# High parts of the woven stage's weights: rounded by a casting transfer of GpSimd's queue instead of by ScalarE, with rings of 5 high and 3 low slots

## The chip, the cores and the metric

The kernel runs on one core of one Trainium2 chip. The metric is the device time of one execution in microseconds (us); of several runs the median is taken. The core's engines are TensorE (PE, with PEld for its weight loads), VectorE (DVE), ScalarE (ACT), GpSimd (POOL) and SyncE (SP), which here issues most transfers; each engine works through its own queue in order and waits there for semaphores of the others.

## The reference, cut to what matters

One layer of a hybrid backbone on 256 latent and 256 context tokens, width 2048, in float32: modulated RMSNorm, one input projection, two token mixers beside one another (a bidirectional RWKV-7 with 16 heads, a bidirectional chunked gated DeltaNet with 8 heads), a gated merge of both, an output projection, a residual, and a SwiGLU network with 5632 hidden columns.

```python
h = modulate(rmsnorm(x, norm1_w[layer]), sh1, sc1)
hc = modulate(rmsnorm(ctx, norm1_w[layer]), csh1, csc1)
...
rw, cv, z, ab, gt = jnp.split(h @ w_in, IN_SPLITS, axis=-1)
...
m = jax.nn.sigmoid(g_a) * (o_a @ p_a) + jax.nn.sigmoid(g_b) * (o_b @ p_b)
return m @ w_out
...
x = x + gt1 * y
x = x + gt2 * swiglu(modulate(rmsnorm(x, norm2_w[layer]), sh2, sc2),
                     ffn_w_gate_up[layer], ffn_w_down[layer])
```

The change touches how the weights of `w_in`, `p_a` and part of `p_b` are made ready for the products.

## The kernel before

Large products run on TensorE in the type fp32r, which keeps fewer bits than float32. To keep precision, each weight W and each input X is split in a high part, W rounded to fp32r, and a low part, W minus the high part. A product is then three matmuls: high W by high X, high W by low X, low W by high X.

The kernel has four stages. The first (until about 120 us) makes the modulation and the normed inputs HX and HC (high and low each) and the narrow low-rank columns. The second is the **woven stage** (L164 in the profile), the subject here. The third is the output projection, with the rest of the merge (L1860 to L1862), and the fourth the feed-forward network (L415 to L438).

In the woven stage some thirty generators, each a chain of single operations, are interleaved: `products` (the large products), `prepare`, `grams`, `inverse`, `values` and `scan` for eight pairs of RWKV heads, `features`, `tokens`, `decays`, `head_grams`, `head_inverse` and `head_scan` for eight DeltaNet heads, the merge, and the rest of the modulation (`ada_early`, `ada_rest`). The class `Weave` orders them when the program is built: it keeps a planned time for each engine (a `Lane`) and each generator, always takes the operation that can start earliest by the plan's costs (ties by rank), and emits it. So the order on TensorE, VectorE, ScalarE, GpSimd and SyncE is fixed by a plan whose costs and delays stand in `LAT`; on the chip each engine follows that order and waits where the plan was too hopeful. All of it is recorded under the line of the one call in `Lane.__getattr__`, L164, and loads under L175.

Weights come in **quarters**: 4 of the 16 blocks of 128 rows of a 128-column strip, a tile of 128 x 512 (256 KB). For each quarter two generators run, at a rank ahead of all others:

- `fetch` takes a raw slot from the ring `raws` (3 slots at first; 6 once the early modulation is done with the other three) and has SyncE load the quarter into it.
- `cast` waits for the planned landing, takes a high slot from `his`, has ScalarE round the raw quarter into it (CAST whi<-wraw), takes a low slot from `los`, and has VectorE subtract (TENSOR_TENSOR wlo<-wraw,whi). Then the raw slot goes back, and `products` may use the pair.

The rings `his` and `los` have 4 slots each, the halves of two tiles whi and two tiles wlo. A quarter's 12 or 24 matmuls (latent tokens alone, or latent and context) use both parts; then both slots go back. The loader asks for up to four quarters ahead of the product that runs.

GpSimd has little to do: for each pair it clears edges of a tile (L896, L900), copies and adds the two directions' keys for the bonus (L928, L930, tile bon), and clears the inverse's work tile.

Of the 399 quarters that are cast this way, 344 are of w_in, 32 of pa (p_a) and 23 of pb (p_b); three of the last are gathered from several strips, with columns of 128 elements.

Of the kernel before, what the change touches and what calls it, by code (L numbers as in the profile page):

```python
# [18 lines left out]
P = 128  # L19
# [4 lines left out]
NH = HID // P  # L24
NPAIR = 8
NGH = 8
DECAY = 0.6065306597126334
NHELD, NB = 10, 10
GATES_A, GATES_B = ((36,0,0,0,0,0,0,0),(0,0,0,0,0,4,0,0))

LAT = dict(dma=3.1, v=1.0, s=1.0, hop=dict(e=0.215, v=0.135, s=0.15, g=0.1), slack=0.1, own=0.09, grp=32, crank=-1, cg=4, into=0.14, back=0.2, cross=0.14, stay=0.0, gpace=1.6)
LNEXP = "natural_log_exp_and_others"
SIGM = "sigmoid_and_others"
UNIT = 64 * 64 + 64
# [78 lines left out]
class Lane:  # L113
# [36 lines left out]
    def __getattr__(self, name):  # L150

        def op(out, *a, **k):
            if name == "preload_act_table_set":
                return Op(self, 1.2, lambda: self.engine.preload_act_table_set(out))
            if name == "dma_start":
                return Op(self, 0.6 if self.each > 0.002 else 0.06, lambda: self.engine.dma_start(out, *a))
            mode = base = None
            if name == "transpose" and len(a) == 2:
                cost, mode = 0.109, "full"
            elif name == "matmul":  # L160
                cost, mode = self.product(out, a)
            else:
                cost, base = self.cost(name, out, a, k), (out.offset // out.ap[0][0], out.shape[0])
            return Op(self, cost, lambda: getattr(self.engine, name)(out, *a, **k), mode, base)  # L164
        return op
# [163 lines left out]
def emit(ctx: ExitStack, tc, A, out, dbg=None):  # L329
# [4 lines left out]
    weave = Weave()  # L334
    dq = Loads(Q)
    e, v, s, g = (Lane(x, fixed, each, LAT["own"], LAT["hop"][n]) for x, fixed, each, n in
                  ((E, 0.0, 0.0, "e"), (V, 0.07, 0.00104, "v"), (S, 0.06, 0.0009, "s"), (G, 0.06, 0.0022, "g")))
# [458 lines left out]

    raws, his, los = quarters("wraw", 3, F32), Ring(quarters("whi", 2, F32R)), Ring(quarters("wlo", 2, F32R))
    turns = [itertools.cycle(t) for t in (raws, his.tiles[:], los.tiles[:])]
    raws, spare = Ring(raws[:3]), raws[3:]

    for b in (pib, mmb, psb, psb, mmb, pab):
# [12 lines left out]
    landed = {}  # L814
# [341 lines left out]
    def fetch(parts, i):  # L1156

        for q, part in enumerate(parts):
            raw = yield raws
            landed[i, q] = raw, weave.now + dq(raw[:, :part.shape[1]], part)  # L1160
            weave.ready("asked", i, q)
            yield 0.0

    def cast(parts, i):

        for q, part in enumerate(parts):
            n = part.shape[1]
            yield "asked", i, q
            raw, at = landed.pop((i, q))
            yield max(0.0, at - weave.now)  # L1170
            hi = yield his
            yield s.copy(hi[:, :n], raw[:, :n])
            lo = yield los
            yield v.tensor_sub(lo[:, :n], raw[:, :n], hi[:, :n].bitcast(F32))
            raws.put(raw)
            casts[i, q] = hi, lo
            weave.ready("cast", i, q)
# [16 lines left out]
    def merge_in():  # L1194

        yield "out", NPAIR - 1
        for what in "KV":
            yield what + "gemm", NGH - 1
        oa = hx.tile([P, 2, 8, T], F32R, tag="ch", name="oa")
# [15 lines left out]
    def merge_gates():  # L1215
# [8 lines left out]
        yield w  # L1224
        yield "gram", NGH - 1
        for t in gts:
# [647 lines left out]
    with tc.manual_schedule(engines={mybir.EngineType.PE, mybir.EngineType.DVE, mybir.EngineType.Activation,  # L1874
# [17 lines left out]
        at = (KT - NB) * NGH // CG  # L1892
        acc = mp.tile([P, 1024], F32, name="acc")
        adds = dict(zip((1, 2, 4, 6, 8, 10, 12, 13), range(KT - NLATE, KT)))
        for j in range(KT):
# [7 lines left out]
            k, a = divmod(j, 4)  # L1903
            raw = zap.tile([P, CG, P], F32, tag="wr", name="wr", bufs=2)
# [4 lines left out]
            if j in adds:  # L1909
                i = adds[j]  # L1910
# [25 lines left out]
    with tc.tile_pool(name="fp", bufs=1, reuse_waits="tile") as fp:  # L1936
# [19 lines left out]
        for j in range(NH):  # L1956
# [6 lines left out]
            g = fp.tile([P, T], F32, tag="g", name="g", bufs=2)  # L1963
# [5 lines left out]
            if 2 <= j < 34:  # L1969

                for a in range(2):
                    c = (j - 2) // 2
                    i = 2 * (j % 2) + a
# [120 lines left out]
```

## Time and profile before

| | us |
|---|---|
| profiled execution, its own time | 2182.99 |
| its span | 2181.2 |
| median of 3 runs | 2189.1 |
| the runs | 2182.12, 2189.1, 2189.5 |

| engine | busy us | share of the span |
|---|---|---|
| TensorE matmul | 2104.2 | 96% |
| TensorE weight load | 1973.0 | 90% |
| VectorE | 1551.6 | 71% |
| ScalarE | 1119.0 | 51% |
| GpSimd | 19.3 | 1% |

The share is a mean over stages with different limits, so the stretch of the woven stage is read by itself. The granted clock of TensorE is 0.989 over the span. Matmuls are pipelined: their times overlap, and a busy TensorE can still have short stalls inside.

### The profile page before, as it was taken

The page shows a single profiled execution, that of the slowest core. Times are in us where ns is not written, and L with a number is a line of the kernel's source. Part 1 is how long each engine was busy: PE and PEld are TensorE (multiplying, and loading weights), DVE is VectorE, ACT ScalarE, POOL GpSimd, SP SyncE. Part 2 cuts the span into 40 slices and gives each one's busy share as a digit, 9 for nine tenths or more (in the row PEclk, how much of TensorE's full clock was granted, in tenths as well). Part 3 has the DMA queues.
Part 4 walks back from the last instruction along what each step waited for, and adds up shares of the span by engine and source line. Part 5 has one row for each costly group of instructions (what it writes and reads, how often), then busy time and mean ns, then how long its engine had stood idle before and what let it go on. Part 6 is the DMA issues. An engine that isn't in the chain of part 4 may idle for free.

```text
span 2181.2 us, 59117 instructions
## 1 busy us (share of the span) xinstructions
PE 2104.2 (96%) x24536; PEld 1973.0 (90%) x24536; DVE 1551.6 (71%) x3305; ACT 1119.0 (51%) x2210; POOL 19.3 (1%) x55
## 2 busy tenths in 40 slices
PE   7999999999999999999999998999999999999997
PEld 4987698888898898998989988999999999999997
DVE  4466599889889976898998777865666665554554
ACT  3246654555555556565565664644444444444443
POOL 0000000000000000000000000000000000000000
PEclk9999999999999999999999999999999999999999
DMA  9966756645565564665653745946777776566665
GB/s 385 410 168 198 228 140 180 188 141 154 164 162 154 159 168 142 188 194 169 173 160 105 218 151 178 306 161 216 242 244 239 242 239 209 195 191 194 196 194 163
DMA packets 276813, 431.14 MB, mean 198 GB/s; under 512 B 119872, under 2 KB 137664, under 8 KB 272192
## 3 DMA queue, kind: packets, MB, share of 16 engines
q1 hardware_dynamic: 262720, 402.19, 60.0%
q10 hardware_dynamic: 13824, 25.17, 3.6%
q8 instruction: 192, 3.15, 0.6%
q14 instruction: 77, 0.63, 0.1%
HBM read 401.50 MB, written 25.77 MB: 196 GB/s over the span
## 4 chain that ended last, share of the span: by engine, by line
PE 80%; DVE 7%; DMA 7%; ACT 3%; issue 2%; SPq 1%; DVEq 0%; ACTq 0%
PE mm L164 27%; PE mm L438 12%; PE mm L437 12%; PE mm L436 12%; PE s L164 6%; PE pa L164 5%; PE pi L164 3%; DVE arena L164 2%; DMA wraw<-w 2%; DVE wlo L164 1%; DMA wraw<-ada_rest 1%; PE mm L529 1%; PE s L579 1%; PE mm L579 1%; ACT whi L164 1%
## 5 line engine op out<-in xcount | busy, mean ns | idle before, releaser
L427 DVE TENSOR_TENSOR wlo<-wraw,whi 128x1024 fp32r<-128x1024 f32 (+1 forms) x264 | 315.0, 1193 | 292.6 <-ACT whi L426 292.4
L426 ACT CAST whi<-wraw 128x1024 fp32r<-128x1024 f32 (+1 forms) x264 | 270.6, 1025 | 386.6 <-PE mm L437 341.7
L164 PE MATMUL mm<-hxh,wlo 128*128 128x256 f32 x1376 | 399.5, 290 | 7.0 <-DVE wlo L164 6.4
L164 PE MATMUL mm<-hxh,whi 128*128 128x256 f32 x1376 | 397.2, 289 | 2.8 <-ACT whi L164 1.8
L164 PE MATMUL mm<-hxl,whi 128*128 128x256 f32 x1376 | 395.7, 288 | 0.0
L438 PE MATMUL mm<-hfh,wlo 128*128 128x256 f32 x1344 | 371.7, 277 | 0.6 <-DVE wlo L427 0.6
L436 PE MATMUL mm<-hfh,whi 128*128 128x256 f32 x1344 | 371.0, 276 | 0.0
L437 PE MATMUL mm<-hfl,whi 128*128 128x256 f32 x1344 | 371.0, 276 | 0.0
L164 ACT CAST whi<-wraw 128x512 fp32r<-128x512 f32 (+1 forms) x399 | 243.1, 615 | 206.1 <-PE mm L164 93.5
L164 DVE TENSOR_TENSOR wlo<-wraw,whi 128x512 fp32r<-128x512 f32 (+1 forms) x399 | 270.4, 680 | 86.0 <-ACT whi L164 82.7
L164 PEld LDWEIGHTS mm<-hxh,wlo 128*128 128x128 f32 x1376 | 260.7, 189 | 17.9 <-DVE wlo L164 9.8
L164 PEld LDWEIGHTS mm<-hxh,whi 128*128 128x128 f32 x1376 | 260.7, 189 | 10.9 <-issue 4.1
L164 PEld LDWEIGHTS mm<-hxl,whi 128*128 128x128 f32 x1376 | 261.1, 190 | 6.5 <-issue 4.1
L438 PEld LDWEIGHTS mm<-hfh,wlo 128*128 128x128 f32 x1344 | 252.3, 188 | 1.1 <-DVE wlo L427 1.0
L437 PEld LDWEIGHTS mm<-hfl,whi 128*128 128x128 f32 x1344 | 252.3, 188 | 0.0
L436 PEld LDWEIGHTS mm<-hfh,whi 128*128 128x128 f32 x1344 | 252.3, 188 | 0.0
L164 PE MATMUL mm<-hch,wlo 128*128 128x256 f32 x496 | 142.3, 287 | 0.0
L164 PE MATMUL mm<-hcl,whi 128*128 128x256 f32 x496 | 142.2, 287 | 0.1
L438 PE MATMUL mm<-za,wlo 128*128 128x256 f32 x512 | 141.4, 276 | 0.1
L436 PE MATMUL mm<-za,whi 128*128 128x256 f32 x512 | 141.5, 276 | 0.0
L437 PE MATMUL mm<-za,whi 128*128 128x256 f32 x512 | 141.3, 276 | 0.0
L164 PE MATMUL mm<-hch,whi 128*128 128x256 f32 x496 | 140.9, 284 | 0.0
(417 smaller groups left out, 4519.8 us busy)
## 6 DMA issues: line engine op xcount, KB each, us to landing
wraw<-w SPq DMA_DIRECT2D x344, 256.0 KB, 3.3
wraw<-wgu SPq DMA_DIRECT2D x168, 512.0 KB, 4.7
aw<-ada_first SPq DMA_DIRECT2D x32, 1024.0 KB, 10.3
wraw<-wdn SPq DMA_DIRECT2D x64, 448.0 KB, 3.7
wraw<-ada_rest SPq DMA_DIRECT2D x96, 256.0 KB, 3.3
aw<-ada_rest SPq DMA_DIRECT2D x48, 512.0 KB, 4.3
wraw<-wout SPq DMA_DIRECT2D x64, 256.0 KB, 5.9
aw<-ada_gt ACTq DMA_DIRECT2D x64, 256.0 KB, 5.2
```

Source lines behind the costliest of these rows:

```text
L164: return Op(self, cost, lambda: getattr(self.engine, name)(out, *a, **k), mode, base)
L426: S.copy(hi[:, c, :M], raw[:, c, :M])
L427: V.tensor_sub(lo[:, c, :M], raw[:, c, :M], hi[:, c, :M].bitcast(F32))
L436: E.matmul(ps, hi, Xh[:, k, :n], start=first and i == 0, stop=False)
L437: E.matmul(ps, hi, Xl[:, k, :n], start=False, stop=False)
L438: E.matmul(ps, lo, Xh[:, k, :n], start=False, stop=last and i == len(wt) - 1)
L529: E.matmul(ps[32 * g:32 * g + 32, 0:P], ckr[:, k].rearrange("p a b -> p (a b)"), aws[e, c][:, i, g], start=k == 0, stop=k == KT - 1)
L579: E.matmul(ps[:m, T * a:T * a + T], w_, X[:, 2 * e + k, :], start=e == k == i == 0, stop=e == NE - 1 and k == 1 and i == len(todo) - 1)
```

## The change

`fetch` now takes a raw slot and a high slot together. It has SyncE load the raw quarter as before, and has GpSimd's queue load the same quarter a second time, into the high slot, with a cast from float32 to fp32r on the way (in pieces of 2 columns of 128 where the quarter is gathered). `cast` loses ScalarE's rounding; VectorE subtracts what was loaded as the high part from what was loaded raw. One slot of the tiles wlo moves from `los` to `his`: 5 high and 3 low slots. The plan counts 1.0 us on GpSimd for such a transfer's issue (`gd`) and 3.5 us until it has landed (`swc`). The casts of the other stages stay with ScalarE, and the output projection keeps its own turns of 4 and 4 slots.

```diff
+MORE = 1
...
-LAT = dict(dma=3.1, v=1.0, s=1.0, hop=dict(e=0.215, v=0.135, s=0.15, g=0.1), slack=0.1, own=0.09, grp=32, crank=-1, cg=4, into=0.14, back=0.2, cross=0.14, stay=0.0, gpace=1.6)
+LAT = dict(dma=3.1, v=1.0, s=1.0, hop=dict(e=0.215, v=0.135, s=0.15, g=0.1), slack=0.1, own=0.09, grp=32, crank=-1, cg=4, into=0.14, back=0.2, cross=0.14, stay=0.0, gpace=1.6, swc=3.5, gd=1.0)
...
-                return Op(self, 0.6 if self.each > 0.002 else 0.06, lambda: self.engine.dma_start(out, *a))
+                return Op(self, LAT["gd"] if self.each > 0.002 else 0.06, lambda: self.engine.dma_start(out, *a))
...
     turns = [itertools.cycle(t) for t in (raws, his.tiles[:], los.tiles[:])]
+    his.tiles += los.tiles[4 - MORE:]
+    los.tiles = los.tiles[:4 - MORE]
+    his.free, los.free = [0.0] * len(his.tiles), [0.0] * len(los.tiles)
     raws, spare = Ring(raws[:3]), raws[3:]
...
             raw = yield raws
-            landed[i, q] = raw, weave.now + dq(raw[:, :part.shape[1]], part)
+            hi = yield his
+            n = part.shape[1]
+            at = weave.now + dq(raw[:, :n], part)
+            step = n if part.ap[-2][0] == P else 2
+            for j in range(0, n, step):
+                yield g.dma_start(hi[:, j:j + step], part[:, j:j + step])
+            landed[i, q] = raw, hi, max(at, weave.now + LAT["swc"])
             weave.ready("asked", i, q)
-            yield 0.0
...
             yield "asked", i, q
-            raw, at = landed.pop((i, q))
+            raw, hi, at = landed.pop((i, q))
             yield max(0.0, at - weave.now)
-            hi = yield his
-            yield s.copy(hi[:, :n], raw[:, :n])
             lo = yield los
             yield v.tensor_sub(lo[:, :n], raw[:, :n], hi[:, :n].bitcast(F32))
```

Since lines are added, L164 of the kernel before is L165 in the changed kernel, and L896 to L930 are L900 to L934. The plan is made anew, so all queues are reordered. Three places show how.

ScalarE's queue before, at the end of the first pair's scan, beside which the second pair's runs (R, VX and gate are tiles of the scan, y of its readout, KB of the grams, arena holds the pairs' work tiles, whi the high part):

```order
L164 COPY R_5244<-s 128x256
L164 COPY VX<-s 64x2x64 x3
L164 CAST whi<-wraw 128x512
L164 COPY VX<-s 64x2x64
L164 CAST whi<-wraw 128x512
L164 COPY VX<-pa 64x4x64 x4
L164 COPY gate<-pa 128x256
L164 COPY VX<-pa 64x4x64 x2
L164 CAST whi<-wraw 128x512
L164 COPY VX<-pa 64x4x64 x2
L164 ACTIVATE y_5407<-Y 128x256
```

The same place in the changed kernel:

```order
L165 COPY R_5120<-s 128x256
L165 COPY KB<-pa 64x2x64 x4
L165 COPY VX<-s 64x2x64 x3
L165 ACTIVATE arena<-arena 128x8x64
L165 COPY VX<-s 64x2x64
L165 ACTIVATE arena<-arena 128x512
L165 COPY VX<-pa 64x4x64 x4
L165 COPY gate<-pa 128x256
L165 COPY VX<-pa 64x4x64 x4
L165 ACTIVATE y_5290<-Y 128x256
```

The three casts between the scan's copies are gone, and activations of the next pair (arena) have moved up beside them.

GpSimd's queue before, in the first pair of heads (bon is the bonus tile):

```order
L896 MEMSET arena 128x8
L928 COPY bon<-arena 128x256
L900 MEMSET arena 128x8
L930 ISA
L930 TENSOR_TENSOR bon<-bon,arena 128x256
```

In the changed kernel the same rows, with the transfers that now stand among them (a high slot that is made of a tile wlo is the ring's fifth):

```order
L932 COPY bon<-arena 128x256
L157 DMA wlo<-w 128x512
L157 DMA whi<-w 128x512 x4
L904 MEMSET arena 128x8
L157 DMA wlo<-w 128x512
L157 DMA whi<-w 128x512 x3
L934 ISA
L934 TENSOR_TENSOR bon<-bon,arena 128x256
```

Every fifth transfer goes to the slot that came from the low ring, and the copy and the sum of the bonus, which wait for VectorE, now have transfers queued behind them.

ScalarE's table loads are placed by the order of its activations. ScalarE's queue before, at the features of one DeltaNet head (arena holds them, 512 columns of k and 768 of v and q):

```order
L164 ACT_TABLE_LOAD
L164 ACTIVATE arena<-arena 128x512
L164 ACTIVATE arena<-arena 128x768
L164 CAST whi<-wraw 128x512
L154 ACT_TABLE_LOAD
L164 ACTIVATE arena<-arena 128x512
```

In the changed kernel, at such a place:

```order
L165 ACT_TABLE_LOAD
L165 ACTIVATE arena<-arena 128x512
L165 ACT_TABLE_LOAD
L165 ACTIVATE arena<-pa 128x512
L165 COPY extra<-pi 32x4x32 x2
L165 ACT_TABLE_LOAD
L165 ACTIVATE arena<-arena 128x768
L155 ACT_TABLE_LOAD
```

An exponential (arena<-pa) now stands between the two activations of the features, and brings a load on each side; over the program there are 42 table loads in place of 34.

## The prediction

> **What bounds the kernel now.** I read the page's head first, then the stage that the change touches as one stretch (165 to 1335 us, nearly all of the woven stage), then what that stage's engines wait for. The columns of a stretch are PE, PEld, DVE, ACT and POOL busy with their instruction counts, then the granted clock, the DMA engines' share and GB/s.
>
> ```profile
> span 2181.2 us, 59117 instructions
> PE 2104.2 (96%) x24536; PEld 1973.0 (90%) x24536; DVE 1551.6 (71%) x3305; ACT 1119.0 (51%) x2210; POOL 19.3 (1%) x55
> ...
> 165.00:1335.00 1170.00, 1130.37 (x15481) 1024.54 (x15480) 968.76 (x2397) 675.35 (x1581) 18.77 (x49) 0.99 0.58 169
> ```
>
> In the stage TensorE is busy 1130.4 of 1170 us, VectorE 968.8 (83%), ScalarE 675.4 (58%), GpSimd 1.6%, the DMA engines 58%. So TensorE bounds the stage, VectorE stands next, and 1170 - 1130.4 = 39.6 us of TensorE's idle time is all that shows as open to a change of this kind. Matmuls overlap, so a short stall between two of them can hide inside the 1130; 39.6 is the visible part.
>
> What ends that idle time is the next view (engine and tile that waited, what it waited for, us in total, times, longest):
>
> ```profile
> PE mm L164 <- DVE wlo L164: 5.7, 10, 1.5
> PE s L164 <- ACT lo L164: 5.4, 5, 1.9
> ...
> PE mm L164 <- ACT ob L164: 2.6, 3, 1.2
> PE s L164 <- DVE Rg L164: 2.3, 3, 1.2
> PE pi L164 <- DVE iv L164: 2.2, 2, 1.2
> PE pa L164 <- ACT arena L164: 2.0, 4, 0.8
> PE s L164 <- ACT VX L164: 1.5, 3, 0.9
> PE s L164 <- ACT R L164: 1.5, 1, 1.5
> PE s L164 <- DVE Vn L164: 1.4, 1, 1.4
> PE pi L164 <- DVE Qm L164: 1.4, 2, 0.8
> PE pi L164 <- DVE arena L164: 1.4, 4, 0.9
> PE pa L164 <- ACT kkn L164: 1.4, 1, 1.4
> ```
>
> Waits that ScalarE ends in these rows: 5.4 + 2.6 + 2.0 + 1.5 + 1.5 + 1.4 = 14.4 us. Waits that VectorE ends: 5.7 + 2.3 + 2.2 + 1.4 + 1.4 + 1.4 = 14.4 us too.
>
> **The change part by part.**
>
> *Removed: ScalarE's casts.* The two groups of the stage (count and first forms | busy, mean ns | idle just before them and what ended it):
>
> ```profile
> L164 ACT CAST whi<-wraw 128x512 fp32r<-128x512 f32 (+1 forms) x379 | 230.9, 615 | 197.6 <-PE mm L164 91.4 <-DMA wraw<-w 62.2 <-issue 17.8
> L164 DVE TENSOR_TENSOR wlo<-wraw,whi 128x512 fp32r<-128x512 f32 (+1 forms) x379 | 256.7, 680 | 82.7 <-ACT whi L164 79.4 <-PE pa L164 0.4 <-issue 0.3
> ```
>
> 379 of the 399 casts lie in the stretch: 230.9 us of work, and 197.6 us in which ScalarE stood before a cast with whatever was queued behind it, since an engine works in order. Both go: 428 us, 37% of the stage, is freed on ScalarE. On the path this is worth at most the 14.4 us that TensorE waits for ScalarE, and at least nothing. Those waits are for copies and activations of the recurrences, and in the order before nearly every second row ahead of them is a cast; after, they stand alone. I take three quarters, **-11 us**; what is late next is VectorE's part of the same chains.
>
> *VectorE's subtraction.* It waited 82.7 us for casts; that wait goes. In its place it waits for the casting transfer, and for the raw load, at the head of its own queue. Behind it in VectorE's queue stand the products of the scans, the masks of the grams and the shifts, and TensorE waits for those. The nearest row for a queue whose head waits on such loads is ScalarE's own: 62.2 us for the landing of raw quarters. I take that value: 82.7 - 62.2 = 20 us less idle on VectorE. What a us of VectorE's idle time costs lies between 14.4 / 201 = 0.07 (TensorE's waits on it, over its 1170 - 968.8 us idle) and 1 (if VectorE were the bound, which at 83% busy it nearly is); I take a third: **-7 us**. The ends are -20 us, and a loss, which is the first rival.
>
> *Added: 401 transfers on GpSimd's queue.* 396 plain quarters and three gathered ones in 2 + 2 + 1 pieces. No run here shows a casting transfer, nor any transfer from this queue. Issue: the nearest rows are SyncE's issue and GpSimd's own work,
>
> ```profile
> L175 SPq DMA_DIRECT2D wraw<-w x321: 327/328/2054, 165.8 to 1202.2; - x161
> ```
>
> ```profile
> 215.01 1.05 POOL L930 TENSOR_TENSOR bon<-bon,arena 128x256 f32<-128x256 f32 x1 [15.94 <-DVE arena L164]
> ```
>
> 0.33 us to some 1.05 us each; 401 at 1.05 us are 421 us of GpSimd's 1170, of which 18.8 are used, so the queue has room and I cost the issue itself at nothing. Landing: loads of the same 256 KB take, from issue,
>
> ```profile
> wraw<-w SPq DMA_DIRECT2D x344, 256.0 KB, 3.3
> ...
> wraw<-wout SPq DMA_DIRECT2D x64, 256.0 KB, 5.9
> ...
> wraw<-pa SPq DMA_DIRECT2D x32, 256.0 KB, 3.0
> ```
>
> 3.0 us on a quiet machine to 5.9 us where the queue is deep. The order is laid out for 1.0 us of issue and 3.5 us of flight, 4.5 us in all, in the middle of these; I take 4.5, since the stage's 58% lies nearer to the 3.3 us row. The Trainium skill, page "DMA: Bandwidth & Descriptors", section "Anatomy of one DMA — SWDGE (gpsimd) path", gives a fit of 2.0 us + bytes / 436e3 for such a transfer, an estimate of 2.6 us for 256 KB; by it the landing would never be the late part, and VectorE's term would be the whole -20 us times its third, the same -7 us. No run here shows it.
>
> *Slots.* A high slot is now taken when its load is asked for, not at the cast, so it is held some 4 us longer; for that the ring has 5 in place of 4. A ring of 5 with 4.5 us of flight, 0.68 us of subtraction, a few tenths of hops and a use of about 3 us turns in about 9 us, 1.8 us a quarter; the stage needs one in 1170 / 379 = 3.1 us. Only where runs of 12 matmuls follow close on one another, as in the merge (start, us, what, from the chain),
>
> ```profile
> 1247.72 1.29 PE mm L164 x11
> 1249.46 1.27 PE mm L164 x11
> 1251.17 1.28 PE mm L164 x11
> ```
>
> one quarter in 1.7 us, there is no margin, and a late landing shows at once. That is at most the 32 quarters of pa out of 379, so nothing in the sum. The three low slots are held from subtraction to last matmul only, so they stand for two quarters ahead of TensorE; I cost them at nothing, with the same cover, and at the first rival's price if it is gone.
>
> *GpSimd's older work.* Copies and sums of the bonus (L928, L930) and the clears now stand between transfers, and wait for VectorE. A transfer behind such a copy goes out as late as VectorE is. Eight pairs have two each, 16 waits in all; with five slots a us of lateness there is covered by two quarters, so nothing.
>
> *Start.* Now the first quarter is cast and used while the DMA engines are at 95% (the two instructions, the last low-rank matmuls of the chain, and two stretches):
>
> ```profile
> 124.59 0.62 ACT L164 CAST whi<-wraw 128x512 fp32r<-128x512 f32 x1 [0.57 <-DMA wraw<-w]
> 125.26 0.38 PE L164 MATMUL mm<-hxh,whi 128*128 128x256 f32 x1 [0.68 <-ACT whi L164]
> ```
>
> ```profile
> 136.28 0.72 PE pa L579 x6
> ```
>
> ```profile
> 110.00:130.00 20.00, 18.58 (x246) 17.16 (x245) 11.85 (x31) 7.73 (x15) 0.00 (x0) 1.00 0.95 201
> 130.00:150.00 20.00, 19.29 (x166) 18.90 (x165) 12.63 (x30) 9.25 (x17) 0.11 (x1) 1.00 0.39 118
> ```
>
> After, a high part can only be asked for when the last use of its slot in the low-rank part is over, and lands 4.5 us later, where a cast took 0.6. TensorE has low-rank matmuls until 137 us, which hide most of it: **+3 us**, between 0 and 4.
>
> *Table loads.* The new order has 42 loads of ScalarE's function tables where 34 were, because activations of different sets now meet more closely.
>
> ```profile
> L154 ACT ACT_TABLE_LOAD x14 | 18.0, 1283 | 0.2
> L164 ACT ACT_TABLE_LOAD x14 | 18.0, 1283 | 0.2
> ```
>
> 8 x 1.28 = 10 us on an engine that has 428 us freed; **+1 us**, between 0 and 10.
>
> **Sum:** -11 - 7 + 3 + 1 = -14 us against the profiled execution's own 2182.99 us (2181.2 of span): 2169. The runs shown are 2182.12, 2189.1 and 2189.5, so their median lies 6.1 us above it; a median of runs of the changed kernel should lie a few us above 2169. I say **2172**.
>
> **The rivals.**
>
> *Nothing to measure: ScalarE was not on the path.* It was 58% busy, TensorE 97%. If the freed time only lets ScalarE wait for TensorE earlier (its rows say so: 91.4 us of its waits before casts are for TensorE's slots), then -11 becomes -3 and the VectorE term zero: 2184. Against it stand the 14.4 us that TensorE does wait for ScalarE.
>
> *Slower: the landing becomes VectorE's wait.* Place: the subtraction, at the head of VectorE's queue. Point of decision: a mean wait of over 82.7 / 379 = 0.22 us per subtraction loses. Price: now ScalarE waits 65 times for a slot and 39 times for a landing in this stretch:
>
> ```profile
> ACT whi L164 <- PE mm L164: 91.4, 65, 4.9
> ACT whi L164 <- DMA wraw<-w: 62.2, 39, 3.2
> ```
>
> After, a late slot means a late landing, so take 104 subtractions that are laid out right at the landing. If it takes 5.9 us (the row of wout) in place of 4.5, each waits 1.4 us more: 104 x 1.4 + 62.2 - 82.7 = +125 us of VectorE idle, a third of it 42; with -11, +3 and +1 that is +35: 2218. For it: the next case's load on the DMA engines. Against it: on average two quarters lie ready ahead of TensorE.
>
> *Slower still: the DMA engines fill up.* A 256 KB quarter costs, by this stretch,
>
> ```profile
> 1375.00:1430.00 55.00, 55.00 (x485) 54.83 (x484) 46.30 (x77) 33.23 (x62) 0.00 (x0) 1.00 0.89 294
> ```
>
> (the output projection, with the same 256 KB loads beside little else) 294 / 0.89 = 330 GB/s, 0.79 us of all sixteen. 379 of them add 300 us, 0.26 of the stage: 0.58 becomes 0.84, still below the top. If a casting packet took twice a plain one's time, 0.52 would come on top, 1.10, and the stage would be 10% longer, 117 us: 2300. The Trainium skill, "DMA: Bandwidth & Descriptors", section "Issuing engines are not separate DMA queues", says that transfers from GpSimd run on the same 16 DMA engines as SyncE's and interleave with them; by it the 0.26 must be added, as I do, and nothing is gained by a second queue but issue time. No run here shows what a cast costs there.
>
> *The change does not do what it says.* If the transfer did not round, the times above would be the same, so this is no case of its own.
>
> **How the numbers follow.** Forecast (2172) 0.40; nothing to measure (2184) 0.30; landing on VectorE (2218) 0.22; full DMA engines (2300) 0.08. Low end: all of the visible 39.6 us of TensorE's idle time gone from 2183, about 2143. High end: the first slower rival with a little more, 2222; above it I leave the last rival's 0.08 and some of the other's. What a measurement of this kernel can tell from no change is about 0.5%, 11 us. Faster by more than that 0.40, within it 0.30, slower 0.22 + 0.08 = 0.30.
>
> **What would show it.** Right: in the stretch 165 to 1335 ScalarE's busy time falls to about 450 us, the waits of TensorE on ScalarE fall below 5 us, VectorE's wait before the subtractions is about 62 us and named after a transfer, the DMA share is about 0.84, transfers from GpSimd land in about 3.5 us. Wrong: a wait before the subtractions of 150 us or more (first slower rival), a DMA share near 1 with landings of 6 us and more (second), or TensorE's idle time unchanged with ScalarE's gone (nothing). The forecast moves the stage's end by 14 us and leaves everything behind it as it is, where the output projection keeps its old four and four slots.

## The result, and the profile after

The changed kernel takes 2312.7 us (median of 6 runs, 2305.0 to 2318.7) where the kernel before takes 2187.0 (6 runs, 2182.1 to 2189.5): a ratio of 1.0575, 95% interval 1.0547 to 1.0603. It is 126 us slower; 2172 us, and at most 2222, was predicted.

The head of the page of the changed kernel, two of its rows over forty slices of the span, its first two DMA queues, and the shares of the chain that ended last:

```profile
span 2303.3 us, 59315 instructions
PE 2148.2 (93%) x24536; PEld 2004.5 (87%) x24536; DVE 1555.8 (68%) x3305; ACT 908.2 (39%) x1819; POOL 238.8 (10%) x456
...
PEclk9999998999999999999999989999999999999999
DMA  9999788787887978786778987683777777666665
...
q1 hardware_dynamic: 262720, 402.19, 56.6%
q0 software_dynamic: 58384, 103.83, 16.9%
...
PE 59%; DMA 20%; DVE 11%; issue 6%; ACT 2%; SPq 1%; POOL 1%; DVEq 0%; ACTq 0%; POOLq 0%
```

The row of the DMA engines and the shares of the chain on the page before:

```profile
DMA  9966756645565564665653745946777776566665
...
PE 80%; DVE 7%; DMA 7%; ACT 3%; issue 2%; SPq 1%; DVEq 0%; ACTq 0%
```

TensorE runs the same 24536 matmuls; its idle time is 2303.3 - 2148.2 = 155 us in place of 77, and it counts 44 us more as busy. In the chain, transfers rise from 7% to 20%, and ScalarE, which the change relieves, was only 3% of it before. The row of the DMA engines has a higher digit in nearly every slice of the first 25, the woven stage, and runs on behind them as before, only later: the loss lies in that stage. There, in the stretch that the prediction read, and in a longer one that holds about the same number of TensorE's instructions as the first did before:

```profile
165.00:1335.00 1170.00, 1074.86 (x14299) 963.76 (x14297) 899.44 (x2207) 439.50 (x1127) 202.73 (x386) 0.96 0.82 231
165.00:1460.00 1295.00, 1181.54 (x15538) 1062.92 (x15536) 978.85 (x2410) 477.18 (x1215) 226.50 (x429) 0.96 0.81 230
```

What took 1170 us now takes about 1295. For about the same work ScalarE is busy 477 us in place of 675, as planned. TensorE is busy for 91% of the longer stretch, where it was 97% before, and VectorE for 76%, where it was 83%: the stage waits more. The DMA share has risen from 0.58 to 0.82. What that does to a transfer is in the view of DMA issues (count, KB each, median us from issue to landing), first before, then after, both for 165 to 1335 us:

```profile
wraw<-w SPq DMA_DIRECT2D x321, 256.0 KB, 3.3
scr<-arena SPq DMA_DIRECT2D x32, 128.0 KB, 3.1
scr<-LT SPq DMA_DIRECT2D x16, 64.0 KB, 2.7
```

```profile
wraw<-w SPq DMA_DIRECT2D x323, 256.0 KB, 4.5
whi<-w POOLq DMA_DIRECT2D x257, 256.0 KB, 4.7
scr<-arena SPq DMA_DIRECT2D x32, 128.0 KB, 4.6
scr<-LT SPq DMA_DIRECT2D x16, 64.0 KB, 5.4
```

The casting transfers land in 4.7 us, near the 4.5 that the plan allows them from the issue on. But the raw quarters, which nobody touched, land 1.2 us later too, and the small round trips through DRAM that the recurrences make (scr) 1.5 to 2.7 us later. VectorE waits for them at the head of its queue, and TensorE behind VectorE (who waited, for what, total us, times, longest; 165 to 1335 us, after):

```profile
DVE wlo L165 <- PE mm L165: 58.5, 63, 10.0
DVE wraw L165 <- DMA wraw<-ada_rest: 48.9, 27, 6.3
DVE wlo L165 <- DMA wraw<-w: 28.9, 25, 3.7
PE mm L165 <- DVE wlo L165: 19.2, 20, 4.1
...
DVE wlo L165 <- DMA whi<-w: 7.9, 10, 2.0
...
PE pa L165 <- ACT kkn L165: 7.5, 2, 6.3
```

TensorE's wait for the low part was 5.7 us before and is 19.2. VectorE's wait for the modulation's loads (ada_rest) was 14.4,

```profile
DVE wraw L164 <- DMA wraw<-ada_rest: 14.4, 11, 3.5
```

and is 48.9. For 58.5 us the subtraction waits for TensorE to give back one of the three low slots. For the new transfers themselves it waits only 7.9 us. How such a stall looks in the chain (start us, us, what):

```profile
319.26 0.70 DVE wlo L165
319.96 0.02 issue
319.98 5.20 DMA wraw<-w
...
325.30 0.70 DVE wlo L165
326.01 0.02 issue
326.02 5.08 DMA wraw<-w
...
331.23 0.69 DVE wlo L165
```

Twice here a subtraction frees a raw slot, the next raw load starts at once and lands 5.1 to 5.2 us later, and the subtraction of that quarter follows. One turn of a slot takes 6.0 us, so three raw slots supply a quarter every 2.0 us and no faster. The stage needs one every 3.5 us on the average (336 in 1170 us), so this binds only where quarters with few matmuls follow close on one another.

### The profile page after: what moved, and what is told of

Same layout as the page of the kernel before. It is cut to its first block, busy times and chain, and to the rows that moved or that the text cites. A ratio compares the mean times of both kernels' runs of the same rounds, so it can differ in the third digit from the quotient of the medians.

```text
span 2303.3 us, 59315 instructions
## 1 busy us (share of the span) xinstructions
PE 2148.2 (93%) x24536; PEld 2004.5 (87%) x24536; DVE 1555.8 (68%) x3305; ACT 908.2 (39%) x1819; POOL 238.8 (10%) x456
## 3 DMA queue, kind: packets, MB, share of 16 engines
q0 software_dynamic: 58384, 103.83, 16.9%
## 4 chain that ended last, share of the span: by engine, by line
PE 59%; DMA 20%; DVE 11%; issue 6%; ACT 2%; SPq 1%; POOL 1%; DVEq 0%; ACTq 0%; POOLq 0%
PE mm L165 14%; PE mm L439 11%; PE mm L437 11%; PE mm L438 11%; DMA wraw<-w 5%; DMA wraw<-ada_rest 4%; DVE arena L165 3%; PE s L165 3%; PE pa L165 3%; DVE wlo L165 3%; DMA whi<-w 2%; PE pi L165 2%; DMA wraw<-wgu 2%; DMA tscr<-arena 1%; DMA iv<-tscr 1%
## 5 line engine op out<-in xcount | busy, mean ns | idle before, releaser
L165 PE MATMUL mm<-hxh,wlo 128*128 128x256 f32 x1652 | 447.2, 293 | 23.9 <-DVE wlo L165 23.5
L165 PEld LDWEIGHTS mm<-hxh,wlo 128*128 128x128 f32 x1652 | 307.0, 193 | 37.6 <-DVE wlo L165 29.3
L165 PE MATMUL mm<-hxh,whi 128*128 128x256 f32 x1100 | 320.4, 291 | 4.4 <-issue 2.4
L165 PE MATMUL mm<-hxl,whi 128*128 128x256 f32 x1100 | 318.7, 290 | 0.0
L165 DVE TENSOR_TENSOR wlo<-wraw,whi 128x512 fp32r<-128x512 f32 (+1 forms) x319 | 217.6, 683 | 104.7 <-PE mm L165 48.3
L157 POOL DMA_DIRECT2D whi<-w x275 | 146.8, 534 | 860.9 <-PE mm L165 516.5
L165 PEld LDWEIGHTS mm<-hxh,whi 128*128 128x128 f32 x1100 | 212.6, 193 | 8.7 <-issue 4.0
L165 PEld LDWEIGHTS mm<-hxl,whi 128*128 128x128 f32 x1100 | 212.8, 193 | 7.2 <-issue 4.9
L165 PE MATMUL mm<-hch,wlo 128*128 128x256 f32 x592 | 173.1, 298 | 0.4 <-issue 0.4
L165 DVE TENSOR_TENSOR arena<-arena 128x512 f32<-128x512 f32 (+17 forms) x522 | 120.6, 232 | 23.7 <-DMA arena<-scr 9.5
L165 PEld LDWEIGHTS mm<-hch,wlo 128*128 128x128 f32 x592 | 115.0, 194 | 5.3 <-issue 3.7
```

The source lines that it names most:

```text
L157: return Op(self, LAT["gd"] if self.each > 0.002 else 0.06, lambda: self.engine.dma_start(out, *a))
```

## The experiments

Times are given as the ratio to the kernel before, run beside it on the same chip, with its 95% interval. "In the order of before" means that every engine executes its rows in the order that it had there, but for a few rows around the stage's start and end; the quarter of the bytes keeps the order of the changed kernel in the same way. All other edits make the planner lay out the stage anew. The theories that the expectations name are T, that the added traffic is the cost, and in each run a rival of its own.

### Are the added bytes the loss?

**A second load of every quarter** (kernel before; SyncE loads each quarter once more into DRAM that nothing reads; order of before):

```
+    sink = itertools.cycle([dpool.tile([P, CG, P], F32, name=f"sink{i}") for i in range(8)])
...
+            Q.dma_start(next(sink)[:, :part.shape[1]], part)
```

> The kernel before, with its order and its casts by ScalarE; SyncE loads each quarter of the woven stage a second time, into memory that nobody reads. Nothing waits for the second transfer. Theory T (traffic): the 104 MB that the change adds make every load of the stage land later (raw quarters 3.3 us before, 4.5 after), and that is what costs; then this kernel is slower too, 2250 to 2310 us, with raw quarters landing in 4.3 us or more. Theory S (slots and supply: the high slot held from the request on, the ring too short, three low slots): 2180 to 2200 us, since the rings are the old ones.

Measured 2414.1 us, ratio 1.1065 (1.0999 to 1.1130). Far above what either theory said. The row of the DMA engines over the stretch from 165 to 1335 us shows that the copies, DRAM to DRAM, keep them at 90% or more in 15 of its 40 slices.

```profile
DMA  9999999999999995645556556565564366655555
```

So it shows what a full queue costs, not what the change's 0.82 costs; SyncE's own queue was also loaded. A gentler dose was needed.

**A quarter of the bytes** (changed kernel, in its own order; the casting transfer brings the first 64 of 256 KB, the rest of the high part is zero and the low part carries the whole weight there):

```
+    for t in his.tiles + los.tiles:
+        V.tensor_scalar(t, ones.unsqueeze(1).to_broadcast([P, CG, P]), 0.0, None, ALU.mult)
...
-            for j in range(0, n, step):
-                yield g.dma_start(hi[:, j:j + step], part[:, j:j + step])
+            for j in range(0, n, step)[:1]:
+                yield g.dma_start(hi[:, j:j + 1], part[:, j:j + 1])
```

> The changed kernel, with its plan, rings and order; the casting transfer brings only the first of a quarter's four blocks (64 KB in place of 256), the other three of the high part stay zero, and VectorE's subtraction puts the whole weight into the low part. So it leaves out part of the split's precision. Added traffic: 26 MB in place of 104. Theory T: 2190 to 2230 us. Theory S: the holds, waits and plan are unchanged and only the landing is some tenths of a us earlier, so 2280 to 2315.

Measured 2214.4 us, ratio 1.015 (1.0096 to 1.0204), as theory T said. It has the order, the rings and the issues of the change (but for two pieces of gathered quarters, and eight zeroings ahead of the stage); three quarters of the bytes are gone, and with them 5.75 - 1.5 = 4.25% (93 us) of the 5.75%. Its stretch and its landings stand between those of before and after:

```profile
165.00:1335.00 1170.00, 1115.53 (x15319) 1008.54 (x15318) 952.37 (x2370) 468.60 (x1199) 220.01 (x419) 0.98 0.69 186
...
wraw<-w SPq DMA_DIRECT2D x323, 256.0 KB, 3.7
...
whi<-w POOLq DMA_DIRECT2D x257, 64.0 KB, 3.5
```

The waits of the same stretch tell which of the change's waits the bytes make:

```profile
DVE wlo L165 <- PE mm L165: 52.6, 58, 10.1
...
DVE wraw L165 <- DMA wraw<-ada_rest: 28.4, 16, 6.0
...
DVE wlo L165 <- DMA wraw<-w: 10.6, 8, 2.5
...
PE mm L165 <- DVE wlo L165: 5.9, 7, 1.9
```

VectorE's waits for the two kinds of raw loads fall from 48.9 to 28.4 and from 28.9 to 10.6 us, and TensorE's for the low part from 19.2 to 5.9, where it was before the change. The wait for the low slots, the longest of VectorE's, hardly falls (58.5 to 52.6), so it is not what the bytes cost.

**Half of the quarters** (changed kernel; quarters with odd q are rounded by ScalarE from the raw buffer):

```
+            if q % 2 == 0:
                 for j in range(0, n, step):
...
+            if q % 2:
+                yield s.copy(hi[:, :n], raw[:, :n])
```

> The changed kernel with every second quarter's high part rounded by ScalarE from the raw buffer again, so that half of the casting transfers go; rings of 5 and 3 as in the change. Theory T, in proportion to the bytes: halfway between 2207 us (casts by ScalarE with rings of 5 and 3) and 2313 us (the change), so 2240 to 2275 us, with a DMA share of the stage near 0.70 and raw quarters landing in 3.7 to 4.1 us. Rival Q (loss only where the DMA engines fill up, so strongly bent): 2205 to 2235 us. Rival F (any casting transfer in the supply costs, whatever the bytes): 2280 us or more.

Measured 2237.5 us, ratio 1.023 (1.0202 to 1.0257), just under the proportional forecast and just over that of a strong bend: with half of the transfers the kernel loses 2.3%, under half of 5.75%, and the rings and a new order are in that too. The DMA share of the stretch is 0.71, and a raw quarter lands in 3.8 us.

**128 KB of traffic from GpSimd's queue** (kernel before; half of each quarter is loaded once more into DRAM that nothing reads, in a new order):

```
+            yield g.dma_start(next(sink)[:, :2], part[:, :2])
```

> The kernel before, with half of each quarter (128 KB) loaded a second time by GpSimd's queue into DRAM that nothing reads. Slots, rings, ScalarE's casts and SyncE's queue are as before; only traffic is added, and GpSimd issues it. Theory T (added traffic alone makes the other loads land later and the stage longer): a DMA share of the stage of 0.70 to 0.85, raw quarters landing in 3.8 to 4.6 us, 2230 to 2300 us. Rival S (the loss lies in the slots and waits that the casting transfer brings, not in its bytes): 2185 to 2210 us.

Measured 2260.3 us, ratio 1.0349 (1.0329 to 1.0370), in theory T's range of times, with a DMA share of 0.67 and raw landings of 3.7 us, both a little under what T said. Because the planner counted the issue and laid out a new order, it was repeated with the planner blind to it, **in the order of before, with 128 KB and with 64 KB**:

```
+            nc.gpsimd.dma_start(next(sink)[:, :2], part[:, :2])
```

> The kernel before in its own order, with half of each quarter (128 KB) loaded a second time by GpSimd's queue into DRAM that nothing reads. In a new order the same traffic took 2260 us. Theory T (the added traffic alone is the cost): 2240 to 2275 us, raw quarters landing in 3.7 us or more. Rival O (most of those 76 us were the new order): 2190 to 2225 us.

> As the run with 128 KB of traffic added in the order of before, with 64 KB instead, so half of its bytes and as many GpSimd transfers. If the cost is by bytes in proportion: half of that run's excess over before, so 2215 to 2230 us if that run takes 2260. If it rises only where the DMA engines fill up: under a third of it, 2185 to 2210 us. If it is by transfers and not by bytes: as that run.

Measured 2247.7 us, ratio 1.0288 (1.0255 to 1.0321), with 128 KB, as T said, and 2207.8, ratio 1.0105 (1.0090 to 1.0119), with 64 KB, a third of the other's excess and under the proportional forecast. No engine but GpSimd itself waits for these transfers, they hold no slot, the casts are ScalarE's and the order is that of before. Stretch, queue and raw landings with 64 KB, then with 128 KB:

```profile
165.00:1335.00 1170.00, 1122.02 (x15323) 1015.05 (x15322) 954.98 (x2370) 667.22 (x1564) 208.71 (x414) 0.98 0.64 186
...
q0 software_dynamic: 11680, 23.94, 7.5%
...
wraw<-w SPq DMA_DIRECT2D x323, 256.0 KB, 3.7
```

```profile
165.00:1335.00 1170.00, 1099.78 (x14868) 991.01 (x14867) 931.90 (x2312) 653.37 (x1529) 210.16 (x414) 0.97 0.68 202
...
q0 software_dynamic: 17520, 47.86, 13.4%
...
wraw<-w SPq DMA_DIRECT2D x326, 256.0 KB, 3.9
...
DVE wraw L164 <- DMA wraw<-ada_rest: 32.5, 23, 4.7
```

Such traffic raises the same landing, and with 128 KB the same wait, as the change does, and lengthens the stage with the DMA engines at 0.64 and 0.68, well below full. The price bends upward: 64 KB take 0.075 x 1170 = 88 us of DMA time and cost 21 us, GpSimd's issue included; the next 64 KB take 69 more with as many issues and cost some 40.

### Slots and rings

**The old casts with the new rings** (kernel before with 5 high and 3 low slots):

```
+    his.tiles += los.tiles[3:]
+    los.tiles = los.tiles[:3]
+    his.free, los.free = [0.0] * 5, [0.0] * 3
```

> The kernel before with rings of 5 high and 3 low slots, casts by ScalarE as they were. Theory T: the rings matter little, 2180 to 2200 us. Theory S in the form that the third low slot is what is missing: 2230 us or more.

Measured 2207.2 us, ratio 1.0117 (1.0063 to 1.0170): a cost of 26 us, between the two expectations, of which the run can't tell the ring from its new order (below).

**The new transfers with the old rings** (changed kernel with MORE = 0, so 4 and 4):

```
-MORE = 1
+MORE = 0
```

> The changed kernel with the rings at 4 and 4. Theory T: within 20 us of the changed kernel's 2313, the traffic being the same. Theory S in the form that high slots are short: 2340 us or more. In the form that low slots are short: 2290 or less.

Measured 2357.3 us, ratio 1.0804 (1.0746 to 1.0863), 45 us above the change, as the theory of short high slots said. The trace agrees: VectorE's subtraction waits 39.9 us for casting transfers in the stretch, 7.9 with five slots, so the fifth high slot is used. But the order is new too, and the 45 us can't be given to the slot alone (below).

**The raw load asked before the high slot is taken** (changed kernel):

```
             raw = yield raws
-            hi = yield his
             n = part.shape[1]
             at = weave.now + dq(raw[:, :n], part)
+            hi = yield his
```

> The changed kernel with one difference: fetch asks the raw load before it waits for a free high slot, so that a raw load no longer waits with the casting transfer for the slot. Theory T (the casting transfers' bytes make every load land later, 4.5 us instead of 3.3 for a raw quarter, and the supply with three raw buffers and the chains through DRAM are bound by that latency): the raw buffers stay the narrow ring, so little changes, 2295 to 2325 us. Rival C (the coupling of the raw load to a high slot makes most of the loss): 2215 to 2270 us, with fewer waits of VectorE's subtraction for the raw load.

Measured 2291.7 us, ratio 1.0475 (1.0435 to 1.0516): 1.0% better than the change, a little below what theory T said and far from what the coupling would give if it were the loss. The raw quarters land no sooner (4.6 us).

### The order of the work

**The planner told the measured latencies** (changed kernel):

```
-LAT = dict(dma=3.1, ... swc=3.5, gd=1.0)
+LAT = dict(dma=4.5, ... swc=4.7, gd=0.53)
```

> The changed kernel with the planner's latencies set to what the trace of the change showed: 4.5 us instead of 3.1 for a load of SyncE's queue, 4.7 instead of 3.5 for a casting transfer, 0.53 instead of 1.0 us for its issue on GpSimd. Only the order of the work changes. Theory T: the latency is physical and the buffers are as many as before, so the order mends little, 2290 to 2330 us. Rival L (the order was laid out for loads that land too soon, so engines wait in program order for late data): 2215 to 2275 us.

Measured 2283.5 us, ratio 1.0433 (1.0400 to 1.0467): 1.4% better, between the ranges of the two theories. **Both mends together:**

> The changed kernel with both mends together: the raw load asked before the high slot is taken (alone 2292 us) and the planner's latencies set to the measured ones (alone 2284 us), against 2313 us for the change. If the two mend different losses, they add: 2255 to 2270 us. If they mend the same one, 2275 to 2295 us. Theory T in either case: above 2240 us, since the bytes stay, with raw quarters still landing in 4.4 to 4.7 us.

Measured 2271.8 us, ratio 1.0400 (1.0365 to 1.0436), between the two ranges of its expectation. The interval overlaps that of the planner's latencies alone, so whether the two add is open; about 70% of the loss stays even so.

**A new order and nothing else** (kernel before, one number of the planner):

```
-LAT = dict(dma=3.1,
+LAT = dict(dma=3.3,
```

> The kernel before with one number of the planner changed: a load is counted with 3.3 us (what its profile shows) instead of 3.1. Same instructions, same bytes, same rings, a new order. If a new order by itself costs what the runs with a new order and little else lost (+13 to +20 us): 2195 to 2210 us. If the order doesn't matter by itself: 2178 to 2192 us.

Measured 2224.7 us, ratio 1.0180 (1.0163 to 1.0198). The same work, bytes and rings in another order, with 46 table loads on ScalarE in place of 34, cost 38 us, where the expectation had 13 to 20. The stretch shows no load on any engine that would explain it, only more idle time on TensorE (63.5 us in place of 39.6):

```profile
165.00:1335.00 1170.00, 1106.46 (x15194) 994.36 (x15194) 941.39 (x2341) 677.06 (x1566) 20.41 (x49) 0.98 0.56 163
```

So the order of before is worth 1.8% over its neighbour, and a difference of 10 to 40 us between two kernels with different orders can't be given to any one edit in them. That holds for the 26 and 45 us of the rings, and for the 1.0% and 1.4% above. It does not hold for the 93 us of the quarter of the bytes, nor for the traffic in the order of before.

### What ScalarE's relief is worth

**A short cast** (kernel before; ScalarE casts 128 of a quarter's 512 columns, and the low part carries the whole weight in the others), first in a new order, where the planner counts the short cast, then in the order of before, where it counts the whole one. The second edit:

```
+    for t in his.tiles + los.tiles:
+        V.tensor_scalar(t, ones.unsqueeze(1).to_broadcast([P, CG, P]), 0.0, None, ALU.mult)
...
-            yield s.copy(hi[:, :n], raw[:, :n])
+            op = s.copy(hi[:, :n], raw[:, :n])
+            op.call = s.copy(hi[:, :1], raw[:, :1]).call
+            yield op
```

> The kernel before (rings of 4 and 4, no second load) with ScalarE's cast cut to the first 128 of a quarter's 512 columns; the rest of each high part stays zero, and the low part carries the whole weight there. It asks what the relief of ScalarE is worth by itself, with nothing paid for it. The prediction's terms for the relief were -11 us (PE's waits for ScalarE) and -7 us (VectorE's wait for the cast). Theory R (the relief is worth that, and the other terms hid it): 2162 to 2178 us. Rival N (the order of the work hides ScalarE's casts anyway, so the relief is worth nothing): 2180 to 2195 us.

> As the run with the short cast (ScalarE casts 128 of a quarter's 512 columns, the rest of the high part is zero), but every engine's instructions stand in the order of before: the planner counts the full cast. Eight zeroings of 0.42 us on VectorE stand ahead of the stage. Theory R (ScalarE's relief is worth the prediction's 11 + 7 us when the order is kept): 2163 to 2176 us, PE's waits for ScalarE in the stage under 5 us and VectorE's wait for the cast near 62. Rival N (the relief is worth nothing, because engines wait for other things in the same places): 2180 to 2190 us.

Measured 2199.3 us, ratio 1.0072 (1.0051 to 1.0093), in the new order, above both ranges that were expected, and 2180.5, ratio 0.9978 (0.9965 to 0.9991), in the order of before. The second is the clean one. Its time lies in the range of the rival that the relief is worth nothing, but its ratio is under 1: the relief gains 0.2%, 5 us. The casts and the wait for them, in the order of before:

```profile
L164 ACT CAST whi<-wraw 128x128 fp32r<-128x128 f32 x379 | 109.6, 296 | 149.6 <-DMA wraw<-w 80.7 <-PE mm L164 42.4 <-DVE arena L164 10.1
```

```profile
DVE wlo L164 <- ACT whi L164: 56.8, 46, 9.7
```

The cast is half as long (296 ns, 615 before), not gone, and ScalarE still waits for landings in front of it. VectorE's wait falls by 79.4 - 56.8 = 23 us, and 5 us of time come of it, with 8 x 0.42 = 3 us paid for the zeroing ahead of the stage.

**The casts on GpSimd, by a copy and not by a transfer** (kernel before), in a new order, where the planner counts GpSimd's copy; in the order of before, where it counts ScalarE's; and in the order of before with the second line below only where q is odd. The second edit:

```
-            yield s.copy(hi[:, :n], raw[:, :n])
+            op = s.copy(hi[:, :n], raw[:, :n])
+            op.call = g.tensor_copy(hi[:, :n], raw[:, :n]).call
+            yield op
```

> The kernel before with one word changed: the copy that rounds the high part runs on GpSimd instead of ScalarE, from the raw buffer, with rings of 4 and 4 and no second load. It takes the casts from ScalarE as the change does, without its bytes, its GpSimd transfers or its shorter low ring. GpSimd's copy of 128x256 took 0.69 us in the profile of before, so a quarter is estimated at 1.3 us, against 0.62 on ScalarE and 3.1 us that PE needs for a quarter. Theory T: with no added bytes the loss of the changed kernel is gone, 2165 to 2200 us, DMA share of the stage 0.58, raw quarters landing in 3.3 us. Rival S (a supply that doesn't go through ScalarE is what loses, since the order of the work was laid around it): 2240 us or more.

> The kernel before in its own order, with the high parts rounded by a copy on GpSimd from the raw buffer (0.80 us a quarter when measured in a new order, where the kernel took 2217 us; ScalarE's takes 0.62). No added bytes, rings of 4 and 4. If the new order was what that run lost (a new order alone lost 38 us): 2176 to 2192 us. If GpSimd's slower cast and VectorE's subtractions beside it (0.72 instead of 0.68 us) were the loss: 2200 to 2220 us.

> As the run with the casts on GpSimd in the order of before, but for every second quarter only; ScalarE keeps the others. Theory: half of the relief (at most 3 us) against half of the slower VectorE work: 2178 to 2190 us, no difference that can be measured. A version faster than both kernels would have to come out under 2176 us.

Measured 2216.9 us, ratio 1.0126 (1.0090 to 1.0163); 2216.1, ratio 1.0158 (1.0134 to 1.0182); and 2192.2, ratio 1.0058 (1.0045 to 1.0072). The first lies between its two ranges, the second in that of slower work on GpSimd and VectorE, the third above what was expected. Without added bytes ScalarE's relief costs more on GpSimd than it brings, and it isn't the order. The two groups in the second of these kernels:

```profile
L164 POOL CAST whi<-wraw 128x512 fp32r<-128x512 f32 x361 | 281.4, 781 | 816.4 <-PE mm L164 512.8 <-DMA wraw<-w 120.2 <-DVE arena L164 54.1
```

```profile
L164 DVE TENSOR_TENSOR wlo<-wraw,whi 128x512 fp32r<-128x512 f32 x360 | 257.8, 719 | 60.8 <-POOL whi L164 44.6 <-issue 8.1 <-DMA sgd__1597<-lo 4.6
```

A cast takes 781 ns (ScalarE's 615), and VectorE's subtraction 719 ns instead of 680. The Trainium skill, page "GPSIMD Engine Reference", section "Specifications", says that GpSimd shares its way into SBUF with VectorE, and contends with VectorE's instructions of two SBUF inputs; the subtraction is one, and its longer time agrees. Which of the two slower operations makes the loss was not separated. No version here that keeps the whole split is faster than the kernel before.

## Why the prediction was wrong

**The removed casts, -11 us, and VectorE's wait, -7 us.** Not refuted and not shown in full. Half of the cast's time, taken away in the order of before, gained 5 us, or 8 with the zeroing taken off; if the other half is worth as much, the whole is 10 to 16, where the two terms had 18. The sign holds and the size is near. In the change the gain is lost among waits that have grown: the subtraction does not wait less (62 forecast), but more,

```profile
L165 DVE TENSOR_TENSOR wlo<-wraw,whi 128x512 fp32r<-128x512 f32 (+1 forms) x319 | 217.6, 683 | 104.7 <-PE mm L165 48.3
L165 DVE TENSOR_TENSOR wlo<-wraw,wlo 128x512 fp32r<-128x512 f32 (+1 forms) x80 | 54.5, 681 | 38.4 <-PE mm L165 14.5 <-DMA wraw<-w 8.5 <-DMA wlo<-pb 7.8
```

The second group is that of the ring's fifth slot. Together they wait 143 us over the whole span, where the 399 subtractions before waited 86.0, and 48.3 + 14.5 = 63 us of it are for the three low slots. TensorE's waits for ScalarE do not fall under 5 us either; that for the tile kkn alone, 1.4 before, is 7.5.

**The issue at nothing, the landing at 4.5 us.** The issue was right:

```profile
L157 POOL DMA_DIRECT2D whi<-w x275 | 146.8, 534 | 860.9 <-PE mm L165 516.5
```

It takes 534 ns a transfer, and GpSimd is busy for 202.7 of the stretch's 1170 us. The landing took 4.7, near the 4.5 of the sum; the 3.5 us that the prediction's last paragraph named as a sign was too short. The Trainium skill's fit of 2.0 us + bytes / 436e3 (page "DMA: Bandwidth & Descriptors", section "Anatomy of one DMA — SWDGE (gpsimd) path") gives 2.6 us for 256 KB and 2.2 for 64 KB, as an estimate; measured were 4.7 and 3.5 beside a stage's other traffic, so the fit can't be used there. GpSimd's older work was rightly put at nothing: in the stretch the only wait of another engine for it is 0.3 us.

**The DMA share: rightly forecast and wrongly priced. This is the step that failed.** The prediction wrote 0.58 + 0.26 = "0.84, still below the top", and gave traffic below the top no price; only an overflow above 1 was to cost time. The measured share is 0.82, and the bytes behind it are most of the loss: with a quarter of them in the same order 93 of the 126 us are gone, and traffic that no other engine waits for costs 21 us at a share of 0.64 and 61 us at 0.68 in the order of before. What the sum lacked is that the loads that were there already land later as the share grows, long before the engines are full: 3.3, 3.7, 3.9 and 4.5 us for a raw quarter at 0.58, 0.64, 0.68 and 0.82 (3.7 at 0.69 with a quarter of the bytes, so it is not the share alone). VectorE waits for them, and TensorE behind it. Everything needed stood in the prediction: landings of 3.0 to 5.9 us for one size, and 62 us of ScalarE's waits for raw loads. The wide landing was applied to the new transfers alone, and not to the old loads beside them.

How the loss divides among the raw ring, the modulation's loads and the round trips is not shown; no run gave the ring another slot. The ring has three slots only until the early modulation is done. The last of its loads goes out at 1051.1 us in the changed kernel and at 981.3 with a quarter of the bytes, beside the same TensorE instruction, so the two kernels are 70 us apart there; at their ends they are 91 apart. Some three quarters of the loss fall in the time of the three slots, but that time is also two thirds of the stage, and the loss goes on with more slots. So three raw slots alone do not explain it.

**The rivals.** The time came out near that of "the DMA engines fill up" (2300), but not by its mechanism; that nearness is luck. A casting quarter takes 0.169 x 2303.3 / 396 = 0.98 us of all sixteen engines (103.83 MB are 396 quarters); SyncE's queue takes 0.566 x 2303.3 / 1534 = 0.85 us for as many bytes, over the whole span and all its sizes of transfer. In the stretch alone, where both run side by side (28.3% for 88.36 MB, 50.8% for 171.46), it is 0.98 and 0.91. So a cast costs 1.08 to 1.16 times as much per byte and not twice, and the share stays under 1. In "the landing becomes VectorE's wait" the place was right, but the late landings were the raw load's (28.9 us) and the modulation's (48.9 us) and not the casting transfer's (7.9 us). The wait before the subtractions of the stretch is 112 us, not the 150 that the prediction named as that rival's sign. The Trainium skill, page "DMA: Bandwidth & Descriptors", section "Issuing engines are not separate DMA queues", says that GpSimd's transfers run on the same 16 engines as SyncE's. The traces agree: SyncE's raw loads land in 4.5 us in place of 3.3.

**Slots at nothing.** Not borne out, and not sized. With four high slots the change loses another 45 us and the subtraction waits longer for its casting transfer, so the fifth slot is used, and it is paid for from the low ring; the new rings alone cost 26 us. Both runs have an order of their own, which may be a large part of either.

**What the sum did not have: the new order itself.** The prediction listed what the new order moves and priced only its table loads. A new order by itself, with its 12 table loads more, cost 38 us in the one run that changed nothing else. What the run with a quarter of the bytes still lost, 1.5% or 33 us, holds the relief, the 64 KB that were left, the rings, the order and 3 us of zeroing. A coarse estimate from the other runs, 21 us for such bytes, 26 for rings and order (of another kernel) and those 3, less 8 to 16 for the relief, makes 34 to 42. How the 26 us divide between the ring of three and the order stays open.

**The start and the table loads** were not tried by themselves; both lie inside that remainder. The start fits its +3 us, as far as two different orders can be compared: TensorE's 2001st instruction starts at 196.8 us, at 194.5 before.

## What to carry to other kernels

Price added traffic by what it does to the loads that are there already, not only by whether the engines overflow. In this stage, which began at a DMA share of 0.58, a further us of DMA time cost a quarter of a us at first (21 for 88) and about a half later (40 for 69). Relief of an engine that made 3% of the last chain was worth little here, and a second load of the same bytes was a high price for it. Where a planner lays out the work, measure a neighbour of the old order first, since an edit that forces a new order pays for the order too; experiments that hold the order fixed tell the two apart.

## What the runs showed of the hardware

A transfer that rounds float32 to float32r took 0.98 us of all sixteen DMA engines for 256 KB, where the mixed transfers of SyncE's queue took 0.91 for as many bytes in the same stretch, and 0.53 us of GpSimd to issue. TensorE's granted clock was lower in most stretches in which it stood idle more; in this one of the changed kernel it was busy for 46 of 55 us:

```profile
330.00:385.00 55.00, 46.00 (x621) 43.22 (x620) 39.12 (x96) 10.33 (x27) 11.81 (x21) 0.89 0.90 243
```

From 935 to 990 us it was busy for 54.5 of 55, and the clock was 1.00; from 165 to 220 us, though, the clock was 1.00 with 48.3 us busy. Over the stage it was 0.96, 0.99 before, so up to 3% of the stage could be matmuls at a lower clock. That is not shown: one of the six runs of the changed kernel had a clock of 0.929 over its span and took 2310.2 us, in the middle of the six, where the others had 0.968 to 0.972. That idle time lowers the clock is read from this coincidence; it was not tried.
